# Gains of the inner norms folded into the split of the transposed output; modulation sums and a rotation product moved from GpSimd to VectorE

## The chip, the cores and the metric

One core of one Trainium2 chip runs the whole program once. The metric is the device time of that execution in microseconds (us): 1910.28 us before, the median of 3 runs (1908.68 to 1917.12). The engines are named as the profile names them: PE (TensorE matmuls), PEld (its weight loads), DVE (VectorE), ACT (ScalarE), POOL (GpSimd), SP (the queue that issues most DMAs).

## The reference, cut to what matters

Four layers run on 512 sample tokens and 128 prompt tokens of width 1024: differential attention, retention, HGRN2, differential attention. Every layer modulates its normed input, projects it, mixes it, norms each head, gates it and projects it back:

```python
for l in range(4):
    shift, scale, gate = split(silu(c) @ w_mod[l] + b_mod[l])   # for c and for c_ctx
    h = rms_norm(x, g_pre[l]) * (1 + scale) + shift
    # attention: q and k of the samples get the axial rotation
    #   x1*cos - x2*sin, x1*sin + x2*cos  on pairs of a head's 64 values
    o = rms_norm(o, da_subln[j]) * (1 - lam_init)    # layers 0 and 3, gain of 128, the same for 8 heads
    o = rms_norm(o)                                  # layer 1, no gain
    o = rms_norm(o, hg_norm)                         # layer 2, gain of 128, the same for 8 heads
    y = (o * silu(g)) @ w_out
    x = x + gate * rms_norm(y, g_post[l])
```

## The kernel before, in words

Activations stand transposed as `hh` and `hl` (8 blocks of 128 features by 640 tokens), a rounded high part and the low rest; weights are split in the same way into `whi` and `wlo`. A product is three matmuls (high by high, high by low, low by high). Each split costs a copy on ACT (the high part) and a subtraction on DVE or POOL (the low part, `lo`, L116).

The order of PE's instructions is written out by hand. In a layer, `weave` alternates the mixer of one head (`main`) with the projections of later heads (`fill`). All other queues (DVE, ACT, POOL, SP) are ordered by the framework's scheduler from its own estimates, so a change of any instruction can shift the order on these four; each queue then runs strictly in that order, so a waiting instruction holds whatever stands behind it.

Four pieces matter here.

**Modulation sums.** `mod_next` (L340 to L369) multiplies rows of `w_mod` into the accumulator `macc`, a row of 128 by 256 for each of two conditioning vectors. In the attention layers odd rows take this way: two ACT copies with a scale make `mpart` (L359, two buffers), and POOL adds it to `macc` (L363, 128 by 512). Even rows are two multiply-adds on DVE (L361). The sums are one chain: each step reads what the last one wrote. Layer 0 has 48 such adds, layer 3 has 16; in layer 1 all of it is on DVE, and layer 2 has none.

**Rotation.** `rope` (L750 to L768): DVE multiplies by the cosine (L757), swaps neighbours with a shuffle (L759), POOL multiplies by the sine (L761), DVE adds (L762), ACT makes the high part (L763), DVE the low (L764). DMAs then rearrange the keys into `kk` and `kz` (L735) and the queries into `qq` (L742), and PE scores them (L783, L784). This runs 32 times in each attention layer.

**Gate.** `gate` (L617 to L625) makes 2 silu(g) with ACT and DVE; in the attention layers and in HGRN2 a POOL product (L625) then multiplies the norm's gain in, from a tile that a DMA has broadcast to all partitions (`sub`, L655, scaled on DVE at L656; `ng`, L1061).

**Transposed output.** `head_out` (L627) scales a head's result by the reciprocal root from POOL (L391) and by the gate into `y` (L637). `y_to_h` (L440) and `y_col` (L492) transpose `y` by 128 columns, so that a head's 128 values lie on partitions, and split the result into `hh` and `hl`: ACT at L431 or L498, DVE at L116.

At the start `setup` loads small parameter rows by DMAs on ACT's queue (L280 to L286), transposes them on PE (L293, L302) and copies them into `par`.

Of the kernel before, what the change touches and what calls it, by code (L numbers as in the profile page):

```python
# [11 lines left out]
F32 = mybir.dt.float32  # L12
# [76 lines left out]
class Net:  # L89
# [187 lines left out]
    def setup(self, sp):  # L277
        nc, t, cp = self.nc, self.t, self.cp
        rows = sp.tile([96, 4, P], F32, name="rows")
        nc.scalar.dma_start(rows[0:8, 0, :], t["c"].rearrange("b (r p) -> (b r) p", p=P))  # L280
        self.ident = self.const(cp, "ident")
        nc.scalar.dma_start(rows[8:16, 0, :], t["c_ctx"].rearrange("(r p) -> r p", p=P))
        nc.scalar.dma_start(rows[:, 1, :], t["b_mod"].rearrange("l (r p) -> (l r) p", p=P))
        nc.scalar.dma_start(rows[0:32, 2, :], t["g_pre"].rearrange("l (r p) -> (l r) p", p=P))
        nc.scalar.dma_start(rows[32:64, 2, :], t["g_post"].rearrange("l (r p) -> (l r) p", p=P))
        nc.scalar.dma_start(rows[0:64, 3, :], t["hg_lb"].rearrange("d l (r p) -> (d l r) p", p=P))  # L286
        self.half = cp.tile([P, NT], F32, name="mhalf")
        nc.vector.memset(self.half, -0.5)
        self.smod = cp.tile([P, KT, 32], F32, name="smod")
        nc.vector.memset(self.smod, 0.0)  # L290
        par = cp.tile([P, 240], F32, name="par")
        pt = self.one()
        nc.tensor.transpose(pt[:, 0:16], rows[:16, 0, :], self.ident[:16, :16])  # L293
        nc.vector.tensor_copy(par[:, 0:16], pt[:, 0:16])
        th = sp.tile([P, 16], F32, name="th")
        nc.scalar.activation(th, par[:, 0:16], AF.Tanh, scale=0.5)
        nc.vector.scalar_tensor_tensor(out=th, in0=th, scalar=1.0, in1=par[:, 0:16], op0=ALU.add, op1=ALU.mult)
        nc.vector.tensor_scalar(out=self.smod[:, :, 0:2], in0=th.rearrange("p (j k) -> p k j", j=2),
                                scalar1=0.5, scalar2=None, op0=ALU.mult)
        pt = self.one()  # L300
        for i, n, o in ((1, 96, 0), (2, 64, 96), (3, 64, 160)):
            nc.tensor.transpose(pt[:, o:o + n], rows[:n, i, :], self.ident[:n, :n])  # L302
        nc.vector.tensor_copy(par[:, 16:240], pt[:, 0:224])
        self.bmodT = par[:, 16:112].rearrange("p (l r) -> p l r", l=4)
        self.gpre = par[:, 112:144].rearrange("p (l r) -> p l r", l=4)
        self.gpost = par[:, 144:176].rearrange("p (l r) -> p l r", l=4)
        self.lbl = par[:, 176:240].rearrange("p (d l r) -> p d l r", d=2, l=4)
# [33 lines left out]
    def mod_next(self, rows):  # L341
# [3 lines left out]
        while self.mod_owed >= 1 and self.modr:  # L345
# [16 lines left out]
            if pool is not None:  # L362
                nc.gpsimd.tensor_tensor(out=self.macc, in0=self.macc, in1=part, op=ALU.add)  # L363
            if 4 * i + k == 5:
# [62 lines left out]

    def put_h(self, src, tt, eng=None, k0=0):
        nc = self.nc
        hi, lo = (a[:, k0:k0 + src.shape[1], TOK[tt]:TOK[tt] + 128] for a in (self.hh, self.hl))  # L430
        nc.scalar.activation(hi, src, AF.Copy)  # L431
        self.lo(lo, src, hi, eng)

# [7 lines left out]
    def y_to_h(self, y, tt, n=KT, m=4):  # L441

        nc = self.nc
        for k0 in range(0, n, m):
            ks = range(k0, min(n, k0 + m))
            pt = self.one([P, 4, P]) if m == 4 else self.two([P, 8, P])
            for k in ks:
                nc.tensor.transpose(pt[:, k - k0, :], y[:, k * 128:k * 128 + 128], self.ident)
            self.put_h(pt[:, 0:len(ks), :], tt, nc.vector, k0)
            yield 0.11 * len(ks)  # L450
# [41 lines left out]
    def y_col(self, y, k):  # L492

        nc = self.nc
        pt = self.two([P, 1024])
        for tt in range(NT):
            nc.tensor.transpose(pt[:, TOK[tt]:TOK[tt] + 128], y[:, tt, k * 128:k * 128 + 128], self.ident)
        a = nc.scalar.activation(self.hh[:, k, :], pt[:, 0:640], AF.Copy)  # L498
        b = self.lo(self.hl[:, k, :], pt[:, 0:640], self.hh[:, k, :], nc.vector)
        return a.ins, b.ins  # L500
# [115 lines left out]

    def gate(self, o, ps, gain=None):  # L617

        nc = self.nc
        nc.scalar.activation(o, ps, AF.Tanh, scale=0.5)  # L620
        nc.vector.scalar_tensor_tensor(out=o, in0=o, scalar=1.0, in1=ps, op0=ALU.add, op1=ALU.mult)
        if gain is not None:
            n = 2 * o.shape[1]
            o = o.rearrange("p t (h e) -> p (t h) e", e=P)
            nc.gpsimd.tensor_tensor(out=o, in0=o, in1=gain.unsqueeze(1).to_broadcast([P, n, P]), op=ALU.mult)  # L625

# [18 lines left out]
    def diff(self, l, y):  # L645
# [3 lines left out]
        with tc.tile_pool(name=f"da{l}", bufs=2, reuse_waits="tile") as mp:  # L649
# [3 lines left out]
            nc.sync.dma_start(lv, t["da_lambda"][j].rearrange("a b -> (a b)").partition_broadcast(P))  # L653
            sub = mp.tile([P, P], F32, bufs=1, name="sub")
            nc.sync.dma_start(sub, t["da_subln"][j].partition_broadcast(P))  # L655
            nc.vector.tensor_scalar(out=sub, in0=sub, scalar1=1.0 - lam_init, scalar2=None, op0=ALU.mult)  # L656
            lp = mp.tile([P, 2, 64], F32, tag="sh", name="lp")
# [7 lines left out]
            nc.vector.tensor_scalar(out=nlam, in0=nlam, scalar1=-lam_init, scalar2=None, op0=ALU.add)  # L665
            st = types.SimpleNamespace(mp=mp, l=l, j=j, cc=cc, cs=cs, sub=sub, nlam=nlam, v={}, sg={}, q={}, k={})
            st.o, st.scored, st.done = {}, -1, -1
# [16 lines left out]
    def diff_part(self, st, kind, p):  # L684
# [13 lines left out]
        def use_g(tr, ps):  # L698
            self.gate(sg[:, tr, :], ps, st.sub)

# [49 lines left out]
    def rope(self, st, c0, hi, lo, pr, scale=1.0):  # L750
# [3 lines left out]
        def use(j, ps):  # L754
# [5 lines left out]
            nc.scalar.activation(pr[:, j * 64:j * 64 + 64], prompts(ps, j), AF.Copy, scale=scale)  # L760
            nc.gpsimd.tensor_tensor(out=sh, in0=sh, in1=st.cs[:, c], op=ALU.mult)  # L761
            nc.vector.tensor_tensor(out=t1, in0=t1, in1=sh, op=ALU.add)  # L762
# [287 lines left out]
    def hg(self, l, y):  # L1050
        nc, tc, t = self.nc, self.tc, self.t
        with tc.tile_pool(name=f"hg{l}", bufs=1, reuse_waits="tile") as mp:
# [3 lines left out]
            for m, n in ((mf, "mf"), (mg, "mg")):  # L1056
                c = mp.tile([P, 640], F32, tag="w0", bufs=5, name="w0")[:, 0:320]
                nc.sync.dma_start(c, t["consts"][:, CWHERE[n][0]:sum(CWHERE[n])])
                nc.vector.tensor_copy(m.rearrange("p a b -> p (a b)"), c)
            ng = mp.tile([P, P], F32, name="ng")  # L1060
            nc.sync.dma_start(ng, t["hg_norm"][0].partition_broadcast(P))  # L1061

# [23 lines left out]
            for z in pz:  # L1086
                nc.vector.memset(z, 0.0)
            st = types.SimpleNamespace(mp=mp, l=l, rs=rs, mf=mf, mg=mg, ng=ng, co=co, pz=pz, iv={}, sg={}, h={})
            for _ in self.hg_proj(st, 0):
# [7 lines left out]
    def hg_proj(self, st, h):  # L1097
        nc, t, mp = self.nc, self.t, st.mp
        if h == 0:
# [3 lines left out]
            def use(tt, ps):  # L1103
                nc.scalar.activation(iv[:, tt, :], ps[:, 0, :], AF.Copy)
                self.gate(sg[:, tt:tt + 1, :], ps[:, 1:2, :], st.ng)

# [6 lines left out]
        else:  # L1113
            p = h // 2
            sg = st.sg[p] = mp.tile([P, NT, 256], F32, tag="sg", bufs=2, name="sg")
            yield from self.narrow(st.l, 4096 + p * 256, lambda tr, ps: self.gate(sg[:, tr, :], ps, st.ng))
        hd = st.h[h] = types.SimpleNamespace(th=[])
# [315 lines left out]
```

## Time and profile before

| | |
|---|---|
| median of 3 runs | 1910.28 us |
| the profiled execution | 1908.83 us, its span 1907.0 us |
| granted clock of TensorE, mean | 0.989 |
| attention of layer 0, mostly | 55 to 400 us |
| retention | 500 to 945 us |
| HGRN2 | 1060 to 1410 us |
| attention of layer 3 | 1500 to 1825 us |

The span is from the first instruction to the last. A row such as `L363 POOL ... macc<-macc,mpart` names the line of the code, the engine, the tile written and the tiles read. "Idle before" is time in which that engine had nothing to run, with what ended it. The chain is followed back from the last instruction, at each step to what released it. An instruction's duration includes any time in which it stood started but blocked.

### The profile page before, as it was taken

To read this page: it belongs to the slowest core of one execution; us is meant where nothing else is said; L and a number is where in the kernel's file an instruction comes from. 1 tells how busy PE (TensorE), PEld (TensorE's weight loads), DVE (VectorE), ACT (ScalarE), POOL (GpSimd) and SP (SyncE) were. 2 spreads that over 40 slices of the span, in tenths; PEclk is the share of its full clock that TensorE was granted. 3 is DMA by queue.
4 is the path that set the end of the run, shared out by engine and by line. 5 is a ranking of instruction groups with operands and counts; after the bars stand their busy time and mean duration, and the time that the engine had idled before them with its cause. 6 is when DMAs were issued, how large, how long until landed. Compare 5 with 4: busy or idle time off the path is not lost.

```text
span 1907.0 us, 32063 instructions
## 1 busy us (share of the span) xinstructions
PE 1814.8 (95%) x12060; PEld 1651.2 (87%) x12060; DVE 1315.7 (69%) x2553; ACT 978.1 (51%) x2271; POOL 503.7 (26%) x419
## 2 busy tenths in 40 slices
PE   6989999999999999999999999999979989999998
PEld 4888999977888888888878899999978879999976
DVE  5768788857788998774334667676764766667754
ACT  3456666555444344433343456666654545655552
POOL 0414343202222222222101323342431521222101
PEclk9999999999999999999999999999989999999999
DMA  9644445414345445433323222222214463443322
GB/s 323 177 114 133 133 138 144 128 57 155 126 133 168 140 143 157 142 124 101 104 99 111 85 70 73 64 62 73 62 42 138 132 172 89 112 115 88 107 72 101
DMA packets 231963, 224.59 MB, mean 118 GB/s; under 512 B 11664, under 2 KB 201984, under 8 KB 231808
## 3 DMA queue, kind: packets, MB, share of 16 engines
q1 hardware_dynamic: 231344, 222.16, 38.7%
q8 instruction: 95, 1.56, 0.4%
q14 instruction: 60, 0.49, 0.1%
q10 hardware_dynamic: 464, 0.39, 0.1%
HBM read 174.79 MB, written 18.35 MB: 101 GB/s over the span
## 4 chain that ended last, share of the span: by engine, by line
PE 57%; DVE 20%; ACT 8%; DMA 5%; issue 4%; POOL 3%; SPq 2%; DVEq 0%; ACTq 0%; POOLq 0%
PE one L458 7%; PE one L460 7%; PE one L459 7%; PE one L250 4%; PE one L251 4%; PE one L252 4%; DVE macc L361 4%; DVE wlo L116 3%; PE one L821 3%; PE one L225 3%; PE one L226 2%; PE one L227 2%; ACT whi L178 2%; DMA kz<-ks 1%; DVE nm L785 1%
## 5 line engine op out<-in xcount | busy, mean ns | idle before, releaser
L250 PE MATMUL one<-hh,whi 128*128 128x320 f32 x1152 | 365.4, 317 | 9.3 <-ACT qp L760 6.4
L251 PE MATMUL one<-hl,whi 128*128 128x320 f32 x1152 | 357.0, 310 | 0.0
L252 PE MATMUL one<-hh,wlo 128*128 128x320 f32 x1152 | 356.8, 310 | 0.0
L116 DVE TENSOR_TENSOR wlo<-raw,whi 128x1024 fp32r<-128x1024 f32 x192 | 246.4, 1290 | 134.2 <-ACT whi L178 132.9
L458 PE MATMUL one<-whi,hh 128*128 128x512 f32 x744 | 303.0, 407 | 5.8 <-ACT yo L554 2.5
L460 PE MATMUL one<-whi,hl 128*128 128x512 f32 x744 | 296.1, 398 | 1.0 <-DVE hl L116 0.5
L459 PE MATMUL one<-wlo,hh 128*128 128x512 f32 x744 | 295.6, 397 | 0.0
L178 ACT ACTIVATE whi<-raw 128x1024 fp32r<-128x1024 f32 x192 | 201.3, 1056 | 138.4 <-PE one L251 52.0
L250 PEld LDWEIGHTS one<-hh,whi 128*128 128x128 f32 x1152 | 217.6, 189 | 12.0 <-ACT qp L760 6.8
L361 DVE SCALAR_TENSOR_TENSOR macc<-mraw,smod,macc 128x256 f32<-128x256 f32 x432 | 216.3, 544 | 10.2 <-POOL macc L363 9.6
L251 PEld LDWEIGHTS one<-hl,whi 128*128 128x128 f32 x1152 | 217.6, 189 | 0.5
L252 PEld LDWEIGHTS one<-hh,wlo 128*128 128x128 f32 x1152 | 217.3, 189 | 0.3 <-DVE wlo L116 0.3
L225 PE MATMUL one<-whi,hh 128*128 128x256 f32 x720 | 207.8, 289 | 0.0
L226 PE MATMUL one<-wlo,hh 128*128 128x256 f32 x720 | 201.1, 279 | 0.0
L227 PE MATMUL one<-whi,hl 128*128 128x256 f32 x720 | 201.1, 279 | 0.0
L458 PEld LDWEIGHTS one<-whi,hh 128*128 128x128 f32 x744 | 141.3, 190 | 38.5 <-DVE p L1007 4.0
L460 PEld LDWEIGHTS one<-whi,hl 128*128 128x128 f32 x744 | 140.8, 189 | 37.1 <-DVE hl L116 2.3
L459 PEld LDWEIGHTS one<-wlo,hh 128*128 128x128 f32 x744 | 141.3, 190 | 29.4
L363 POOL TENSOR_TENSOR macc<-macc,mpart 128x512 f32<-128x512 f32 x64 | 94.7, 1481 | 180.9 <-ACT macc L359 65.3
L391 POOL TENSOR_TENSOR rs<-ms,mhalf 128x1 f32<-128x1 f32 (+1 forms) x72 | 66.0, 917 | 288.3 <-DVE ms L384 152.9
L225 PEld LDWEIGHTS one<-whi,hh 128*128 128x128 f32 x720 | 135.5, 188 | 1.5
L226 PEld LDWEIGHTS one<-wlo,hh 128*128 128x128 f32 x720 | 135.6, 188 | 0.0
(344 smaller groups left out, 3765.0 us busy)
## 6 DMA issues: line engine op xcount, KB each, us to landing
mraw<-in_w_mod SPq DMA_DIRECT2D x96, 512.0 KB, 4.2
raw<-in_da_w_in SPq DMA_DIRECT2D x56, 512.0 KB, 4.2
raw<-in_hg_w_in SPq DMA_DIRECT2D x36, 512.0 KB, 3.8
raw<-in_ret_w_in SPq DMA_DIRECT2D x64, 256.0 KB, 3.1
kk<-ks SPq DMA_DIRECT2D x64, 160.0 KB, 3.4
kz<-ks SPq DMA_DIRECT2D x64, 160.0 KB, 3.2
qq<-q SPq DMA_DIRECT2D x64, 128.0 KB, 3.5
raw<-in_da_w_out SPq DMA_DIRECT2D x16, 512.0 KB, 3.5
```

The lines of the kernel that those rows point to most:

```text
L116: return (eng or self.nc.gpsimd).tensor_tensor(out=out, in0=full, in1=hi.bitcast(F32), op=ALU.subtract)
L178: self.nc.scalar.activation(hi, raw, AF.Copy)
L225: mm(out, xh, wh[:, k % 4, :], start=(first and k == ks[0]), stop=False)
L226: mm(out, xh, wl[:, k % 4, :], start=False, stop=False)
L227: mm(out, xl, wh[:, k % 4, :], start=False, stop=(last and k == ks[-1]))
L250: nc.tensor.matmul(ps, wh[:, k, :], self.hh[:, k, c], start=(k == 0), stop=False)
L251: nc.tensor.matmul(ps, wh[:, k, :], self.hl[:, k, c], start=False, stop=False)
L252: nc.tensor.matmul(ps, wl[:, k, :], self.hh[:, k, c], start=False, stop=(k == KT - 1))
L361: nc.vector.scalar_tensor_tensor(out=m, in0=raw[:, k, :], scalar=c, in1=m, op0=ALU.mult, op1=ALU.add)
L458: mm(ps, xh, wh, start=(first and k == ks[0]), stop=False)
L459: mm(ps, xh, wl, start=False, stop=False)
L460: mm(ps, xl, wh, start=False, stop=(last and k == ks[-1]))
```

## The change

Three edits. The gains `hg_norm` and `da_subln` are loaded as three more parameter rows at the head of ACT's DMA queue, transposed with the others, and become per-partition columns (`gains`); those of the attention are scaled by 1 - lam_init there. The POOL product in `gate` and the three broadcast tiles go; instead the split of the transposed output applies the gain, as the scale of ACT's copy and as the scalar of a DVE multiply-subtract. L363's add and L761's product are issued on DVE instead of POOL.

```diff
 def setup(self, sp):
+        nc.scalar.dma_start(rows[64:65, 3, :], t["hg_norm"])
+        nc.scalar.dma_start(rows[65:67, 3, :], t["da_subln"])
         nc.scalar.dma_start(rows[0:8, 0, :], t["c"].rearrange("b (r p) -> (b r) p", p=P))
...
-        for i, n, o in ((1, 96, 0), (2, 64, 96), (3, 64, 160)):
+        for i, n, o in ((1, 96, 0), (2, 64, 96), (3, 67, 160)):
...
+        self.gains = par[:, 240:243]
+        for l in (0, 3):
+            g = self.gains[:, 1 + SLOTS[l]:2 + SLOTS[l]]
+            nc.vector.tensor_scalar(out=g, in0=g, scalar1=1.0 - (0.8 - 0.6 * math.exp(-0.3 * l)), scalar2=None, op0=ALU.mult)
 def mod_next(self, rows):
-                nc.gpsimd.tensor_tensor(out=self.macc, in0=self.macc, in1=part, op=ALU.add)
+                nc.vector.tensor_tensor(out=self.macc, in0=self.macc, in1=part, op=ALU.add)
+    def cut_h(self, hi, lo, src, gain, eng):
+        if gain is None:
+            return self.nc.scalar.activation(hi, src, AF.Copy), self.lo(lo, src, hi, eng)
+        a = self.nc.scalar.activation(hi, src, AF.Copy, scale=gain)
+        return a, eng.scalar_tensor_tensor(out=lo, in0=src, scalar=gain, in1=hi.bitcast(F32), op0=ALU.mult, op1=ALU.subtract)
 def y_to_h(self, y, tt, n=KT, m=4):
-            self.put_h(pt[:, 0:len(ks), :], tt, nc.vector, k0)
+            self.put_h(pt[:, 0:len(ks), :], tt, nc.vector, k0, self.gain)
 def y_col(self, y, k):
-        a = nc.scalar.activation(self.hh[:, k, :], pt[:, 0:640], AF.Copy)
-        b = self.lo(self.hl[:, k, :], pt[:, 0:640], self.hh[:, k, :], nc.vector)
+        a, b = self.cut_h(self.hh[:, k, :], self.hl[:, k, :], pt[:, 0:640], self.gain, nc.vector)
 def gate(self, o, ps):
-        if gain is not None:
-            n = 2 * o.shape[1]
-            o = o.rearrange("p t (h e) -> p (t h) e", e=P)
-            nc.gpsimd.tensor_tensor(out=o, in0=o, in1=gain.unsqueeze(1).to_broadcast([P, n, P]), op=ALU.mult)
 def diff(self, l, y):
-            sub = mp.tile([P, P], F32, bufs=1, name="sub")
-            nc.sync.dma_start(sub, t["da_subln"][j].partition_broadcast(P))
-            nc.vector.tensor_scalar(out=sub, in0=sub, scalar1=1.0 - lam_init, scalar2=None, op0=ALU.mult)
+            self.gain = self.gains[:, 1 + j:2 + j]
 def rope(self, st, c0, hi, lo, pr, scale=1.0):
-            nc.gpsimd.tensor_tensor(out=sh, in0=sh, in1=st.cs[:, c], op=ALU.mult)
+            nc.vector.tensor_tensor(out=sh, in0=sh, in1=st.cs[:, c], op=ALU.mult)
 def hg(self, l, y):
-            ng = mp.tile([P, P], F32, name="ng")
-            nc.sync.dma_start(ng, t["hg_norm"][0].partition_broadcast(P))
+            self.gain = self.gains[:, 0:1]
```

In retention `gain` is None and the split stays as it was. `gate`'s callers drop the argument.

## Rows read from the trace of the kernel before

**Rows 1.** The page: busy time of each engine; the chain by engine.
```profile
PE 1814.8 (95%) x12060; PEld 1651.2 (87%) x12060; DVE 1315.7 (69%) x2553; ACT 978.1 (51%) x2271; POOL 503.7 (26%) x419
...
PE 57%; DVE 20%; ACT 8%; DMA 5%; issue 4%; POOL 3%; SPq 2%; DVEq 0%; ACTq 0%; POOLq 0%
```

**Rows 2.** Busy time by stretch: layer 0, HGRN2, layer 3; then clock, DMA share, GB/s.
```profile
55.00:400.00 345.00, 323.56 (x2366) 311.55 (x2365) 273.31 (x569) 207.95 (x582) 122.92 (x101) 0.99 0.48 136
...
1060.00:1410.00 350.00, 335.46 (x2770) 327.43 (x2771) 240.27 (x360) 218.12 (x425) 117.50 (x85) 0.99 0.23 69
...
1500.00:1825.00 325.00, 312.92 (x2329) 303.25 (x2328) 225.11 (x485) 178.53 (x493) 81.33 (x70) 1.00 0.43 116
```

**Rows 3.** The chain by line, in the stretch 55 to 400 us.
```profile
by line: issue 7.2%; PE one L821 6.9%; DMA kz<-ks 6.1%; DVE nm L785 5.4%; PE one L225 4.7%; PE one L227 4.3%; PE one L226 4.3%; DVE macc L361 3.9%; DVE wlo L116 3.8%; POOL macc L363 3.3%; ACT pe L787 2.9%; SPq L735 2.7%; PE one L811 2.3%; A
```

**Rows 4.** The same from 60 to 100 us and from 1505 to 1555 us.
```profile
by line: issue 13.6%; DMA qq<-q 12.5%; DMA raw<-in_da_w_in 9.7%; POOL sg L625 8.8%; DMA kz<-ks 7.6%; DMA v<-in_cache_v 7.2%; DVE t L762 6.9%; DVE macc L361 6.9%; DVE sh L759 4.5%; DVE wlo L116 4.2%; SPq L735 3.7%; POOL macc L363 3.3%; DVE t
...
by line: POOL macc L363 13.6%; issue 11.7%; DVE macc L361 8.3%; POOL sh L761 7.8%; DMA ck<-in_cache_k 7.2%; DMA mraw<-in_w_mod 6.9%; SPq L735 5.9%; DVE sh L759 5.3%; DVE wlo L116 4.7%; DVE t L757 3.9%; DVE t L762 3.3%; PE one L460 2.4%; PE 
```

**Rows 5.** POOL's groups, layer 0 then layer 3: count | busy us, mean ns | idle before.
```profile
L363 POOL TENSOR_TENSOR macc<-macc,mpart 128x512 f32<-128x512 f32 x48 | 70.3, 1465 | 155.2 <-ACT macc L359 59.3 <-ACT mpart L359 43.7 <-DVE macc L361 31.0
L761 POOL TENSOR_TENSOR sh<-sh,c_ropes 128x256 f32<-128x256 f32 x32 | 30.2, 946 | 67.0 <-DVE sh L759 49.0 <-DVE rc L861 17.9
...
L761 POOL TENSOR_TENSOR sh<-sh,c_ropes 128x256 f32<-128x256 f32 x32 | 34.1, 1065 | 117.8 <-DVE sh L759 64.0 <-DVE ms L389 31.8 <-DVE rc L861 19.0
L363 POOL TENSOR_TENSOR macc<-macc,mpart 128x512 f32<-128x512 f32 x16 | 24.4, 1527 | 25.7 <-DVE macc L361 11.1 <-ACT macc L359 6.0 <-DVE sub L656 5.1
```

**Rows 6.** Waits of ACT, layer 0: us in total, times, longest.
```profile
ACT mpart L359 <- POOL macc L363: 19.7, 20, 2.8
```

**Rows 7.** DVE's groups in layer 0: count | busy us, mean ns | idle before.
```profile
L116 DVE TENSOR_TENSOR wlo<-raw,whi 128x1024 fp32r<-128x1024 f32 x30 | 42.3, 1417 | 3.2 <-ACT whi L178 3.1
L361 DVE SCALAR_TENSOR_TENSOR macc<-mraw,smod,macc 128x256 f32<-128x256 f32 x72 | 35.6, 530 | 2.9 <-POOL macc L363 2.9
...
L762 DVE TENSOR_TENSOR t<-t,sh 128x256 f32<-128x256 f32 x32 | 20.5, 643 | 1.1 <-POOL sh L761 1.1
L862 DVE SCALAR_TENSOR_TENSOR rc<-sums,nlam,rc 128x1 f32<-128x1 f32 x36 | 16.2, 449 | 0.8
...
L116 DVE TENSOR_TENSOR hl<-one,hh 128x512 fp32r<-128x512 f32 x5 | 3.4, 682 | 0.0
```

**Rows 8.** Durations of four of these groups in layer 0: ns min/median/max, first and last start.
```profile
L116 DVE TENSOR_TENSOR wlo<-raw,whi x30: 1199/1221/2326, 59.3 to 383.6; 128x1024 fp32r<-128x1024 f32 x30
L361 DVE SCALAR_TENSOR_TENSOR macc<-mraw,smod,macc x72: 465/474/970, 62.5 to 343.9; 128x256 f32<-128x256 f32 x72
L762 DVE TENSOR_TENSOR t<-t,sh x32: 399/414/1532, 75.2 to 384.8; 128x256 f32<-128x256 f32 x32
L862 DVE SCALAR_TENSOR_TENSOR rc<-sums,nlam,rc x36: 203/220/1256, 105.8 to 396.0; 128x1 f32<-128x1 f32 x36
```

**Rows 9.** Groups of the whole run: a DVE sum of 640, ACT copies with and without scale.
```profile
L1150 DVE TENSOR_TENSOR w<-c 128x640 f32<-128x640 f32 x32 | 25.1, 820 | 0.8
...
L400 ACT ACTIVATE xh<-xt,rs 128x1024 f32<-128x1024 f32 x15 | 17.2, 1149 | 16.8 <-POOL rs L391 16.8
...
L398 ACT ACTIVATE xh<-xt 128x1024 f32<-128x1024 f32 x15 | 15.9, 1059 | 16.8 <-DVE xt L604 16.5
```

**Rows 10.** The gate's products on POOL, whole run.
```profile
L625 POOL TENSOR_TENSOR sg<-sg,sub 128x256 f32<-128x256 f32 (+1 forms) x28 | 28.6, 1027 | 79.9 <-DVE sg L621 71.5 <-DVE modT L334 6.5 <-DMA v<-in_cache_v 1.9
...
L625 POOL TENSOR_TENSOR sg<-sg,ng 128x256 f32<-128x256 f32 (+1 forms) x14 | 18.1, 1297 | 33.6 <-DVE sg L621 28.9 <-DVE lmx L1069 4.7
```

**Rows 11.** Timeline of the start: start us, us, instruction.
```profile
4.85 0.53 ACTq L286 DMA_DIRECT2D rows<-in_hg_lb  x1
...
10.43 0.36 PE L302 MATMUL one<-c_ident,rows 64*128 64x64 f32 x1 [2.42 <-DMA rows<-in_hg_lb]
...
17.08 1.93 PE L1288 MATMUL two<-mraw,smod 128*32 128x256 f32 x16 [2.74 <-DMA mraw<-in_w_mod]
```

More of the change, by code (lines that the diff above doesn't have):

```diff
@@ L290, in setup @@
         nc.vector.memset(self.smod, 0.0)
-        par = cp.tile([P, 240], F32, name="par")
+        par = cp.tile([P, 243], F32, name="par")
         pt = self.one()
@@ L300, in setup @@
         pt = self.one()
-        for i, n, o in ((1, 96, 0), (2, 64, 96), (3, 64, 160)):
+        for i, n, o in ((1, 96, 0), (2, 64, 96), (3, 67, 160)):
             nc.tensor.transpose(pt[:, o:o + n], rows[:n, i, :], self.ident[:n, :n])
-        nc.vector.tensor_copy(par[:, 16:240], pt[:, 0:224])
+        nc.vector.tensor_copy(par[:, 16:243], pt[:, 0:227])
+        self.gains = par[:, 240:243]
+        for l in (0, 3):
+            g = self.gains[:, 1 + SLOTS[l]:2 + SLOTS[l]]
+            nc.vector.tensor_scalar(out=g, in0=g, scalar1=1.0 - (0.8 - 0.6 * math.exp(-0.3 * l)), scalar2=None, op0=ALU.mult)
         self.bmodT = par[:, 16:112].rearrange("p (l r) -> p l r", l=4)
@@ L426, in enter, with put_h @@
         return step
-    def put_h(self, src, tt, eng=None, k0=0):
+    def put_h(self, src, tt, eng=None, k0=0, gain=None):
         nc = self.nc
         hi, lo = (a[:, k0:k0 + src.shape[1], TOK[tt]:TOK[tt] + 128] for a in (self.hh, self.hl))
-        nc.scalar.activation(hi, src, AF.Copy)
-        self.lo(lo, src, hi, eng)
+        self.cut_h(hi, lo, src, gain, eng)
+    def cut_h(self, hi, lo, src, gain, eng):
[3 more added lines that the diff above has]
+        return a, eng.scalar_tensor_tensor(out=lo, in0=src, scalar=gain, in1=hi.bitcast(F32), op0=ALU.mult, op1=ALU.subtract)
     def norm(self, pool, ssq):
@@ L614, in out_layer, with gate @@
                         self.turn(op, l + 1, tt + 3, xh[tt + 3])
-    def gate(self, o, ps, gain=None):
+    def gate(self, o, ps):
         nc = self.nc
@@ L665, in diff @@
             nc.vector.tensor_scalar(out=nlam, in0=nlam, scalar1=-lam_init, scalar2=None, op0=ALU.add)
-            st = types.SimpleNamespace(mp=mp, l=l, j=j, cc=cc, cs=cs, sub=sub, nlam=nlam, v={}, sg={}, q={}, k={})
+            st = types.SimpleNamespace(mp=mp, l=l, j=j, cc=cc, cs=cs, nlam=nlam, v={}, sg={}, q={}, k={})
             st.o, st.scored, st.done = {}, -1, -1
@@ L698, in use_g @@
         def use_g(tr, ps):
-            self.gate(sg[:, tr, :], ps, st.sub)
+            self.gate(sg[:, tr, :], ps)
         def use(tt, ps):
@@ L868, in ret @@
         with tc.tile_pool(name=f"re{l}", bufs=1, reuse_waits="tile") as mp:
+            self.gain = None
             rx = self.const(mp, "rx")
@@ L1087, in hg @@
                 nc.vector.memset(z, 0.0)
-            st = types.SimpleNamespace(mp=mp, l=l, rs=rs, mf=mf, mg=mg, ng=ng, co=co, pz=pz, iv={}, sg={}, h={})
+            st = types.SimpleNamespace(mp=mp, l=l, rs=rs, mf=mf, mg=mg, co=co, pz=pz, iv={}, sg={}, h={})
             for _ in self.hg_proj(st, 0):
@@ L1104, in use @@
                 nc.scalar.activation(iv[:, tt, :], ps[:, 0, :], AF.Copy)
-                self.gate(sg[:, tt:tt + 1, :], ps[:, 1:2, :], st.ng)
+                self.gate(sg[:, tt:tt + 1, :], ps[:, 1:2, :])
             yield from self.proj_a(st.l, 0, use)
@@ L1115, in hg_proj @@
             sg = st.sg[p] = mp.tile([P, NT, 256], F32, tag="sg", bufs=2, name="sg")
-            yield from self.narrow(st.l, 4096 + p * 256, lambda tr, ps: self.gate(sg[:, tr, :], ps, st.ng))
+            yield from self.narrow(st.l, 4096 + p * 256, lambda tr, ps: self.gate(sg[:, tr, :], ps))
         hd = st.h[h] = types.SimpleNamespace(th=[])
```

## The prediction

> **What bounds the kernel now.** I read the page first, then busy time by stretch, then the chain of the stretches that the edits touch, then the groups of POOL and DVE there, and last the spread of single DVE instructions.
>
> The page says that PE is busy for 95% of the span and carries 57% of the chain; DVE follows with 20%, and POOL has 3% [rows 1]. So the most that any edit off PE can return is PE's idle time in the stretches it touches. By stretch that is 345 - 323.56 = 21.4 us in layer 0, 325 - 312.92 = 12.1 us in layer 3 and 350 - 335.46 = 14.5 us in HGRN2 [rows 2]; 33.5 us in the two attention layers.
>
> Layer 0 differs from the other two: its chain is hardly PE. Its first entries are time in which nothing shown was waited for, the value products, the transfer of the keys (6.1%) and DVE's maximum; POOL's add L363 has 3.3% and DVE's half of the same sum 3.9% [rows 3]. In the two starts, POOL weighs more: the gate's product has 8.8% of the 40 us from 60 us on; the add 13.6% and the rotation's product 7.8% of the 50 us from 1505 us on [rows 4]. These are the pieces that the change takes away.
>
> Two further readings say why POOL is dear here. The add takes 1465 ns on average in layer 0, and ACT stands for 19.7 us before `mpart` until the add has freed one of its two buffers [rows 5, 6]; what stands behind it in ACT's queue (the copies that PE's value products need) stands as well. And DVE's instructions in layer 0 come in two kinds: the 128x1 scalar product L862 takes 220 ns as a median, 449 ns as a mean and 1256 ns at worst; L762 has 414, 643 and 1532 [rows 7, 8]. An instruction on one element doesn't take a microsecond by itself; about one POOL instruction is added to it.
>
> **The change part by part.** I make the sum against the profiled execution, 1908.83 us with a span of 1907.0; the median shown is 1.45 us above it.
>
> *POOL's pieces on the chain.* In layer 0 the add has 3.3% of 345 us = 11.4 us [rows 3]. In the start of layer 3 the add has 13.6% of 50 us = 6.8 us and the sine product 7.8% = 3.9 us; the gate's product has 8.8% of 40 us = 3.5 us in the start of layer 0 [rows 4]. Together 25.6 us.
>
> *What DVE takes for them.* The nearest row for an add of 128x512 is DVE's subtraction of the same size, 682 ns [rows 7]; its one operand from PSUM is the difference, and the bounds are 414 ns, the median for half the size from SBUF [rows 8], and 820 ns, the sum of 640 from SBUF [rows 9]. I take 682, the same size. The sine product is a DVE instruction of 128x256 like L762: 414 ns [rows 8], between 399, its minimum, and 682. So the 11.4 us become 11.4 x 682 / 1465 = 5.3, the 6.8 us become 6.8 x 682 / 1527 = 3.0, and the 3.9 us become 3.9 x 414 / 1065 = 1.5 [rows 5]; the gate's 3.5 us go altogether. The chain loses 25.6 - 9.8 = 15.8 us.
>
> [...]
>
> *DVE's load.* New on DVE are 48 + 16 adds, 64 x 0.682 = 43.6 us, and 32 + 32 products, 64 x 0.414 = 26.5 us: 70.1 us in all, 46.0 in layer 0 and 24.1 in layer 3. What DVE gets back is the time in which it stood blocked beside POOL. In layer 0, mean less median times count gives 30 x 196 = 5.9 us (weights' low part), 72 x 56 = 4.0 (L361), 32 x 229 = 7.3 (L762) and 36 x 229 = 8.2 (L862): 25.4 us in four groups [rows 7, 8]. For layer 3 I scale by POOL's moved time, (24.4 + 34.1) / (70.3 + 30.2) = 0.58 [rows 5], which gives 14.8 us, an estimate. So 40.2 us come back at least, bounds 0 (the spread has another cause) and 70 (smaller groups have it too). The load rises by 70.1 - 40.2 = 29.9 us; 9.8 of it is already counted on the chain, and the other 20.1 delay the chain at DVE's share of it, 20% [rows 1]: +4.0 us. DVE's busy time in layer 0 becomes 273.3 + 46.0 - 25.4 = 294 of 345 us [rows 2], 85% instead of 79%: still not the bound.
>
> [...]
>
> *Waits that go.* The 19.7 us of ACT before `mpart` [rows 6] become waits for DVE's add, shorter but behind DVE's queue. I count nothing for it: it is the margin against the next late thing, the transfer of the keys at 6.1% of layer 0's chain [rows 3], which no edit shortens.
>
> *The gate's product.* Off POOL go 28.6 us in the attention layers, counted above where they were on the chain, and 18.1 us in HGRN2 [rows 10]. There PE has 14.5 us of idle time in 350 us [rows 2]; I take a tenth, -1.5 us, between 0 and -5.
>
> *The split with a gain.* Per gained layer 12 splits (ten of `y_to_h`, two of `y_col`), 36 in all. ACT's copy with a column as scale costs 1149 - 1059 = 90 ns more [rows 9]; on DVE a multiply-subtract in place of a subtraction is bounded by 0 and, from L361's 474 ns against L762's 414, by 60 ns [rows 8]. At 150 ns together two or three splits of a layer are waited for by PE, the others run beside the mixer: 8 x 0.15 = +1.2 us. If none was covered it would be 36 x 0.15 = 5.4 us.
>
> *The start.* Two more DMAs stand ahead of `c` on ACT's queue, each about 0.5 us of issue by the 0.53 us of the last one; PE's third parameter transpose waits for that last one until 10.43 us [rows 11]. A delay of 1 us there is covered by PE's wait of 2.74 us for the modulation weights before 17.08 us [rows 11]. +0.5 us; if the cover was gone, 3. Two small DVE scalings and three DMAs less on SP, a scaling of `sub` less on DVE: one against the other, nothing, hidden behind the same transfers.
>
> Sum: -15.8 + 4.0 - 1.5 + 1.2 + 0.5 = -11.6, so 1908.8 - 11.6 = 1897.2: **1897 us**, 0.7% below the median.
>
> **The rivals.**
> - *PE and the keys' transfer hide it.* Layer 0's chain is made of many short pieces with a second one close behind; 95% of PE [rows 1] speaks for it. If two thirds of the 15.8 us are taken up by what is late next, -11.6 + 10.5 = -1.1: 1908 us. The starts of both layers, where POOL itself stands on the chain for microseconds, speak against it.
> - *The blocked time was on the chain.* The return of 40 us on DVE shortens pieces that lie on it now. If all 70 us of relief come and ACT's 19.7 us of waits count for a third, the +4.0 becomes 0 and 6.6 more go: -11.6 - 4.0 - 6.6 = -22.2, 1887 us, still within PE's 33.5 us of idle time.
> - *DVE waits in its own queue.* This ends slower. POOL could stand before an add until ACT had made both halves of `mpart` at no cost; DVE can't, for the scores' maximum and the combination stand behind the add, and PE behind those. POOL did stand: 59.3 and 43.7 us in layer 0 by ACT's copies [rows 5], though mostly where nothing was due. If each of 64 adds holds DVE for a time w, and half of that reaches the chain (layer 0 is 85% full), the price is 32 w. At w = 1 us, near the 1.06 us of an ACT copy [rows 9], it is +32: 1929 us; at w = 0.7 it is about +22 and the kernel is just slower by 0.5%. Against it: the scheduler knows ACT's work and can place the add after it.
> - *It doesn't do what it says.* The scheduler orders the four queues anew for the whole program, so layers that no edit touches can move by a few us either way. That alone gives 1904 to 1914 us.
>
> **How the numbers follow.** About 0.5%, 9.6 us, is what a measurement of this kernel can tell from no change: 1900.7 and 1919.8 us are the bounds of same. Forecast 0.45 (three quarters of it below 1900.7), blocked time on the chain 0.2, hidden 0.15, a new order alone 0.1, DVE waiting 0.1 (all of it slower by over 0.5%). Faster: 0.34 + 0.2 + a little of the rest = 0.57; slower 0.10; same 0.33. The range takes the second rival with the add at its lower bound (64 x 0.268 = 17.2 us less on DVE, 3.4 us at 20%) and HGRN2's -5 in place of -1.5, 1887 - 3.4 - 3.5 = 1880, and the hidden case with the uncovered start and splits, 1908 + 2.5 + 4.2 = 1914; left out are DVE waiting and some of both tails.
>
> **What would show it.** Right: no L363, L761 or L625 on POOL; the add near 682 ns and the product near 414 on DVE; L862's mean falling from 449 to under 260 ns; ACT's waits before `mpart` well under 19.7 us; PE's idle time in layers 0 and 3 down by 12 us together, HGRN2 by 1 or 2. Wrong: DVE idle before the add with ACT named as the releaser (the third rival); medians unchanged but the keys' transfer or SP's queue larger on layer 0's chain (the first); L862 still reaching a microsecond beside a POOL that runs nothing but L391.

## The result, and the profile after

The changed kernel takes 1884.26 us (median of 6 runs, 1880.94 to 1888.67), the kernel before 1912.47 beside it (6 runs, 1908.68 to 1917.12): a ratio of 0.9856, 95% interval 0.9839 to 0.9872. That is 28 us, faster as forecast, and inside the range. The profiled execution took 1885.44 us, with a span of 1883.7. The sum was made against the profiled execution before; the two lie 1908.83 - 1885.44 = 23.4 us apart, twice the 11.6 us of the sum.

The page after: busy time of each engine, and the chain by engine (compare [rows 1]).
```profile
PE 1804.6 (96%) x12060; PEld 1650.3 (88%) x12060; DVE 1304.6 (69%) x2681; ACT 980.7 (52%) x2271; POOL 300.2 (16%) x249
...
PE 66%; DVE 15%; ACT 7%; DMA 5%; issue 3%; SPq 2%; POOL 1%; DVEq 0%; ACTq 0%; POOLq 0%
```
POOL loses two fifths of its time. DVE's total does not rise although 128 instructions, some 70 us, are new on it, and its part of the chain falls from 20% to 15%.

Busy time by stretch (us, then PE, PEld, DVE, ACT, POOL with counts, granted clock, DMA share, GB/s): layer 0, the retention layer's middle, HGRN2, layer 3 (compare [rows 2]).
```profile
55.00:400.00 345.00, 338.48 (x2490) 324.39 (x2489) 280.05 (x675) 218.31 (x606) 8.17 (x7) 1.00 0.48 138
...
460.00:760.00 300.00, 289.05 (x1630) 255.69 (x1630) 257.18 (x565) 129.68 (x281) 81.35 (x58) 0.99 0.46 143
...
1060.00:1410.00 350.00, 337.52 (x2766) 329.29 (x2765) 234.82 (x367) 220.59 (x430) 97.46 (x69) 0.98 0.23 67
...
1500.00:1825.00 325.00, 318.65 (x2381) 309.50 (x2381) 229.09 (x539) 179.51 (x503) 8.18 (x7) 1.00 0.40 113
```
PE's idle time goes from 21.4 to 6.5 us in layer 0 and from 12.1 to 6.4 in layer 3. The chain of layer 0, where PE was hardly seen [rows 3], is now PE's matmuls:
```profile
by line: PE one L826 8.5%; PE one L225 8.0%; PE one L226 7.6%; PE one L227 7.6%; PE one L250 6.8%; PE one L251 6.7%; PE one L252 6.7%; PE two L788 4.8%; PE two L789 4.6%; PE one L816 4.1%; issue 3.8%; SPq L740 1.6%; DVE nm L790 1.5%; PE one
```

Single DVE instructions of layer 0 after: ns minimum/median/maximum, first and last start. The first two groups are the new ones; the other three answer to [rows 8] (the old L762, L862 and L361).
```profile
L369 DVE TENSOR_TENSOR macc<-macc,mpart x48: 676/685/695, 66.4 to 332.1; 128x512 f32<-128x512 f32 x48
L766 DVE TENSOR_TENSOR sh<-sh,c_ropes x32: 398/419/428, 78.4 to 366.6; 128x256 f32<-128x256 f32 x32
L767 DVE TENSOR_TENSOR t<-t,sh x32: 405/418/427, 81.4 to 368.4; 128x256 f32<-128x256 f32 x32
L867 DVE SCALAR_TENSOR_TENSOR rc<-sums,nlam,rc x39: 202/219/224, 108.0 to 398.7; 128x1 f32<-128x1 f32 x39
L367 DVE SCALAR_TENSOR_TENSOR macc<-mraw,smod,macc x72: 465/479/489, 67.1 to 330.3; 128x256 f32<-128x256 f32 x72
```
Medians stay, maxima fall onto them: the one-element product from 1256 ns to 224, L767 from 1532 to 427. Below, "blocked time" is what DVE's instructions of a stretch take above the shortest of their own kind, summed over all kinds. It goes from 48.6 to 8.4 us in layer 0 and from 22.0 to 6.1 in layer 3: 56 us returned. What the shortest instruction of a kind waits too is not in it.

Where the time comes from can be read without windows, since PE runs the same matmuls in the same order in every kernel here (one transpose of parameters at the start is three rows longer): the start of the k-th matmul against its start in the kernel before. These are single profiled executions, so the changed kernel ends 23.3 us ahead here, and not the 28 us of the medians.

| kernel | 250th (end of the start) | 500th | 2750th (end of layer 0) | 6250th (end of retention) | 9000th (end of HGRN2) | 11250th (end of layer 3) |
|---|---|---|---|---|---|---|
| changed | +5.3 | -0.6 | -16.2 | -15.6 | -16.8 | -24.1 |
| only the gain | +5.7 | +3.4 | +2.8 | -2.4 | -3.3 | -8.3 |
| only the sums | +0.3 | -4.1 | -11.4 | -10.6 | -9.5 | -15.6 |
| only the sine product | 0.0 | -1.0 | -1.4 | +0.7 | +0.2 | -3.8 |
| changed, idle sums on POOL | +5.1 | +4.9 | +0.8 | +1.4 | -1.5 | -5.5 |

The start loses 5.3 us, layer 0 then gains 21.5, retention and HGRN2 little, layer 3 another 7.3.

### The profile page after: what moved, and what is told of

Same layout as the page of the kernel before. It is cut to its first block, busy times and chain, and to the rows that moved or that the text cites. A ratio compares the mean times of both kernels' runs of the same rounds, so it can differ in the third digit from the quotient of the medians.

```text
span 1883.7 us, 31931 instructions
## 1 busy us (share of the span) xinstructions
PE 1804.6 (96%) x12060; PEld 1650.3 (88%) x12060; DVE 1304.6 (69%) x2681; ACT 980.7 (52%) x2271; POOL 300.2 (16%) x249
## 4 chain that ended last, share of the span: by engine, by line
PE 66%; DVE 15%; ACT 7%; DMA 5%; issue 3%; SPq 2%; POOL 1%; DVEq 0%; ACTq 0%; POOLq 0%
PE one L470 7%; PE one L472 7%; PE one L471 7%; PE one L250 5%; PE one L251 5%; PE one L252 5%; PE one L225 3%; PE one L826 3%; PE one L226 3%; PE one L227 3%; DVE macc L367 3%; DVE wlo L116 2%; PE two L788 2%; PE two L789 2%; PE one L816 1%
## 5 line engine op out<-in xcount | busy, mean ns | idle before, releaser
L116 DVE TENSOR_TENSOR wlo<-raw,whi 128x1024 fp32r<-128x1024 f32 x192 | 235.9, 1234 | 143.9 <-ACT whi L178 143.2
L367 DVE SCALAR_TENSOR_TENSOR macc<-mraw,smod,macc 128x256 f32<-128x256 f32 x432 | 209.1, 527 | 1.3 <-DMA mraw<-in_w_mod 1.1
L472 PEld LDWEIGHTS one<-whi,hl 128*128 128x128 f32 x744 | 141.0, 190 | 34.5 <-DVE hl L444 1.3
L227 PEld LDWEIGHTS one<-whi,hl 128*128 128x128 f32 x720 | 135.1, 188 | 0.0
```

The costliest lines, as they stand in the source:

```text
L116: return (eng or self.nc.gpsimd).tensor_tensor(out=out, in0=full, in1=hi.bitcast(F32), op=ALU.subtract)
L227: mm(out, xl, wh[:, k % 4, :], start=False, stop=(last and k == ks[-1]))
L367: nc.vector.scalar_tensor_tensor(out=m, in0=raw[:, k, :], scalar=c, in1=m, op0=ALU.mult, op1=ALU.add)
L472: mm(ps, xl, wh, start=False, stop=(last and k == ks[-1]))
```

## The experiments

**One part at a time.** Three kernels, each with one of the three edits. Only the gain: the changed kernel with both operations put back on POOL.
```diff
-                nc.vector.tensor_tensor(out=self.macc, in0=self.macc, in1=part, op=ALU.add)
+                nc.gpsimd.tensor_tensor(out=self.macc, in0=self.macc, in1=part, op=ALU.add)
...
-            nc.vector.tensor_tensor(out=sh, in0=sh, in1=st.cs[:, c], op=ALU.mult)
+            nc.gpsimd.tensor_tensor(out=sh, in0=sh, in1=st.cs[:, c], op=ALU.mult)
```


> The kernel before with the first edit alone: gains loaded first on ACT's queue and applied at the split, L363's add and the sine product still on POOL. Theory A (what counts is POOL's work standing on the chain): 2 to 6 us faster from the 46.7 us of products that leave POOL, less about 5 us that the start loses when two DMAs stand ahead of the conditioning vectors, so -4 to +3 us. Theory B (what counts is that DVE is blocked while POOL reads): the products block DVE too, so about the same, -5 to +2 us. The start in the trace tells the cost of the DMAs apart: +5 us at the last modulation matmul as in the full change, or 0 if that is another order of the queues.

Only the sums, in the kernel before (L363):
```diff
-                nc.gpsimd.tensor_tensor(out=self.macc, in0=self.macc, in1=part, op=ALU.add)
+                nc.vector.tensor_tensor(out=self.macc, in0=self.macc, in1=part, op=ALU.add)
```


> The kernel before with L363's 64 adds on DVE and nothing else. Theory A: most of the gain, 12 to 20 us, nearly all of it in layer 0 where 48 of them are. Theory B: the same size, but with DVE's block times down in proportion to POOL's time that goes (94.7 of 188 us), so 12 to 18 us. Rival (DVE waits in its own queue for ACT's two halves): slower, or DVE idle before the add by over 0.5 us each, 32 us.

Only the sine product, in the kernel before (L761):
```diff
-            nc.gpsimd.tensor_tensor(out=sh, in0=sh, in1=st.cs[:, c], op=ALU.mult)
+            nc.vector.tensor_tensor(out=sh, in0=sh, in1=st.cs[:, c], op=ALU.mult)
```


> The kernel before with the sine product on DVE and nothing else, 64 instructions. Theory A: 3 to 8 us faster, since POOL no longer holds the product behind an add; theory B: 2 to 6 us faster. If the order of the queues is what moves the time, layers 1 and 2 move as well, by over 3 us; both theories expect them unchanged within 2 us.

Measured: the gain alone 1904.39 us (ratio 0.9959, 0.9945 to 0.9972), the sums alone 1894.37 (0.9917, 0.9902 to 0.9931), the sine product alone 1901.25 (0.9952, 0.9933 to 0.997), beside 1910.27 for the kernel before. The gains of 5.9, 15.9 and 9.0 us add to 30.8, near the 28 of the whole, and the sums are the largest. The sums came out as expected; the gain and the sine product gained more than either theory allowed them, by a microsecond or more. Since both theories foresaw nearly the same sizes, these runs do not tell them apart. Nor are the parts clean prices: with the gain alone some 5 us are won in the retention layer (table), which that edit does not touch. In the kernel with the sums alone the one-element product of layer 0 reaches 692 ns at worst; with either of the others alone it still reaches 1256 or 1261.

**The place of the two new DMAs.** The changed kernel, with the two loads of gains last on ACT's queue instead of first.
```diff
-        nc.scalar.dma_start(rows[64:65, 3, :], t["hg_norm"])
-        nc.scalar.dma_start(rows[65:67, 3, :], t["da_subln"])
...
         nc.scalar.dma_start(rows[0:64, 3, :], t["hg_lb"].rearrange("d l (r p) -> (d l r) p", p=P))
+        nc.scalar.dma_start(rows[64:65, 3, :], t["hg_norm"])
+        nc.scalar.dma_start(rows[65:67, 3, :], t["da_subln"])
```


> The changed kernel with the two gain DMAs put last on ACT's queue, behind the one for the HGRN2 bounds. If the 5 us that the start loses come from the place of these DMAs, the last modulation matmul of the start comes 4 to 5 us earlier than in the changed kernel; the whole time falls by 4 to 5 us if the attention of layer 0 begins from there, and by under 1.5 us if that attention waits for its own transfers anyway. If it is a new order of DVE's queue at the start, nothing changes.

Measured: 1884.45 us (ratio 0.9863, 0.9849 to 0.9876), no difference from the changed kernel. The 250th matmul comes 3.1 us earlier than there, less than the 4 to 5 expected; of these, 1.5 us are left at the 275th, about as many at the 500th, and none from the 550th on (some 110 us into the run). So a delay of this size at the start is taken up before layer 0 is a third through; by what was not traced.

**ACT's wait without POOL's work moved.** The kernel before, with four buffers for `mpart` instead of two.
```diff
-                part = pool.tile([P, 2, 256], F32, tag="mpart", bufs=2, name="mpart")
+                part = pool.tile([P, 2, 256], F32, tag="mpart", bufs=4, name="mpart")
```


> The kernel before with four buffers of mpart instead of two, the adds still on POOL. It takes away ACT's wait of 19.7 us in layer 0 (and 6.5 us in layer 3) for POOL and leaves POOL's work and DVE's block times as they are. If ACT's wait is what the change took off the chain, 5 to 12 us faster; if it is DVE's block times, within 3 us of the kernel before.

Measured: 1912.85 us (ratio 1.0009, 0.9998 to 1.002). ACT's waits in layer 0 (us in total, times, longest) say why it settles nothing: the 19.7 us for POOL's sum [rows 6] are gone, and a wait for the modulation's weights stands in their place. The order on ACT's queue changed with the edit, and its copies now come ahead of their weights.
```profile
ACT mpart L359 <- DMA mraw<-in_w_mod: 28.2, 14, 5.2
```

**POOL's work without anyone waiting for it.** The changed kernel, with four buffers, and for each sum on DVE an idle one on POOL, into a tile that nobody reads; beside it the same with four buffers alone.
```diff
                 nc.vector.tensor_tensor(out=self.macc, in0=self.macc, in1=part, op=ALU.add)
+                junk = self.mod_pool.tile([P, 2, 256], F32, tag="mjunk", bufs=1, name="mjunk")
+                nc.gpsimd.tensor_tensor(out=junk, in0=part, in1=part, op=ALU.add)
```


> The changed kernel with four buffers of mpart and, beside each add on DVE, an add of the same size on POOL (mpart plus mpart) into a tile that nobody reads. The result is unchanged; POOL's 64 adds of about 1.3 us are back without anyone waiting for their result. If DVE's block times are what counts, L867 (the scalar product of one element) shows instructions of over 1 us again, DVE is busy for 25 us more in the attention layers, and the time is 6 to 14 us above the same kernel without those adds. If POOL's place on the chain is what counts, the two are within 2 us.

> The changed kernel with four buffers of mpart and nothing else, the base for the kernel with idle adds. Both theories: within 3 us of the changed kernel, since ACT's wait before mpart is already short there.

Measured: 1922.36 us with the idle sums (ratio 1.0057, 1.0036 to 1.0077), 1903.3 without (0.9959, 0.9946 to 0.9973). The control came out 19 us slower than the changed kernel, where at most 3 were expected. The same wait of ACT for weights is there (25.9 us in layer 0), but the order on DVE, ACT and SP moved as well, and in the kernel before, 28.2 us of this wait in place of 19.7 changed nothing; what made the 19 us was not shown. The pair still answers its question, since both have the same order on PE, DVE, ACT and SP: 19 us for POOL work that nobody waits for, more than the 6 to 14 expected. Layer 0 by stretch, with the idle sums and then without:
```profile
55.00:400.00 345.00, 317.90 (x2334) 305.77 (x2332) 285.24 (x640) 202.81 (x566) 64.53 (x54) 0.98 0.47 136
```
```profile
55.00:400.00 345.00, 326.07 (x2384) 313.67 (x2383) 272.04 (x654) 207.53 (x579) 7.06 (x6) 0.98 0.48 138
```
DVE is busy for 13 us more with fewer instructions done (640 for 654), and PE gets through 50 matmuls less.

**The same with nothing else changed.** The two buffers stay, and the idle sum reads the raw weights, so that the buffers of `mpart` come free as in the changed kernel. The buffer of the raw weights is now read by POOL too, but no queue is seen to wait for the idle sum, and ACT's waits for these weights in layer 0 are 2.9 us where the changed kernel has 2.3.
```diff
                 nc.vector.tensor_tensor(out=self.macc, in0=self.macc, in1=part, op=ALU.add)
+                for _ in range(1):
+                    junk = self.mod_pool.tile([P, 2, 256], F32, tag="mjunk", bufs=1, name="mjunk")
+                    nc.gpsimd.tensor_tensor(out=junk, in0=raw[:, k - 1:k + 1, :], in1=raw[:, k - 1:k + 1, :], op=ALU.add)
```


> The changed kernel with one thing more: for each of the 64 sums that went to DVE, POOL adds 128x512 elements of the modulation's raw weights to themselves, into a tile that nobody reads. The order of instructions on PE, DVE, ACT and SP is that of the changed kernel, and no engine waits for the sum. Theory B (POOL's work holds up DVE's instructions beside it, whoever waits for it): the single long DVE instructions come back (the 128x1 product of L867 over 1000 ns at worst), DVE's time above the shortest of each kind in layer 0 goes from 8 to some 30 us, and the kernel loses most of what the pair with four buffers lost for the same work, 19 us: about 1900 us, 1894 to 1906. Theory A (only waits for POOL's results counted): nobody waits, so 1884 us like the changed kernel, within 2.

Measured: 1898.63 us (ratio 0.9938, 0.992 to 0.9955), 14.4 us more than the changed kernel, whose interval lies wholly below. By the table above, layer 0 gives back 17.2 of its 21.5 us and layer 3 3.3 of its 7.3. Durations in layer 0 (minimum/median/maximum; lines are shifted by three):
```profile
L372 POOL TENSOR_TENSOR mjunk<-mraw x44: 1038/1102/2651, 74.1 to 329.1; 128x512 f32<-128x512 f32 x44
```
```profile
L369 DVE TENSOR_TENSOR macc<-macc,mpart x48: 668/681/1190, 66.2 to 348.9; 128x512 f32<-128x512 f32 x48
...
L870 DVE SCALAR_TENSOR_TENSOR rc<-sums,nlam,rc x36: 203/219/999, 111.9 to 396.9; 128x1 f32<-128x1 f32 x36
...
L367 DVE SCALAR_TENSOR_TENSOR macc<-mraw,smod,macc x72: 460/474/1321, 67.0 to 347.1; 128x256 f32<-128x256 f32 x72
```
The long instructions are back, with the order of PE, DVE, ACT and SP unchanged. Blocked time goes from 8.4 to 31.2 us in layer 0 and from 6.1 to 13.0 in layer 3. Theory A, which counts only waits for POOL's results, gave 1884 us and is out as the only cause.

Part of the cost shows as TensorE's clock. In layer 0 the granted clock is at half of full speed for 10.2 us in the kernel before, 3.4 in the changed one and 13.7 with the idle sums (0.99, 1.00 and 0.98 as the mean of the stretch); in the kernel before PE had stood idle for 2.4 to 2.6 us just ahead of each of its three falls, and 3.1 us of idle time at 80 us had no fall behind them. At half speed the 10.2 us that the idle sums add cost at most 5 us, an estimate from these figures.

One of the long instructions in the timeline of this kernel (start us, us, instruction):
```profile
185.20 2.96 POOL L372 TENSOR_TENSOR mjunk<-mraw 128x512 f32<-128x512 f32 x2 [7.95 <-DMA mraw<-in_w_mod]
...
185.75 0.41 DVE L635 SCALAR_TENSOR_TENSOR sg<-sg,one 128x256 f32<-128x256 f32 x1
...
186.08 1.19 DVE L369 TENSOR_TENSOR macc<-macc,mpart 128x512 f32<-128x512 f32 x1
...
187.19 0.99 DVE L870 SCALAR_TENSOR_TENSOR rc<-sums,nlam,rc 128x1 f32<-128x1 f32 x1
```
POOL's pair ends at 188.16 and the one-element product, which needs 0.22 us, at 187.19 + 0.99 = 188.18: it stands until POOL is done. The sum ahead of it, two inputs from SBUF too, stands for half a microsecond. L635, one of whose inputs is in PSUM, takes its usual 0.41 us in the middle of POOL's work. The kernel before shows the same at the sum L363, with a reciprocal of one input that passes unhindered:
```profile
177.30 1.31 POOL L363 TENSOR_TENSOR macc<-macc,mpart 128x512 f32<-128x512 f32 x1 [2.42 <-DVE macc L361]
...
177.36 0.16 DVE L861 RECIPROCAL rc<-sums 128x1 f32<-128x1 f32 x1 [0.21 <-ACT pe L787]
...
177.56 1.06 DVE L862 SCALAR_TENSOR_TENSOR rc<-sums,nlam,rc 128x1 f32<-128x1 f32 x1
```
Two groups of the kernel before part in the same way over all of layer 0. The rotation's sum L762 has two inputs in SBUF: where a POOL instruction runs beside it (12 of 32) it takes 1029 ns on average, elsewhere 411. The product by the cosine L757, of the same size, has one input in PSUM; 15 of its 32 instances run beside POOL, and none is long (compare L762 in [rows 8]):
```profile
L757 DVE TENSOR_TENSOR t<-one,c_ropec x32: 396/414/426, 71.5 to 381.2; 128x256 f32<-128x256 f32 x32
```
The place of the inputs does not explain every case: one instance of L336, with a single input in SBUF, takes 1287 ns there beside a gate's product on POOL and ends 0.03 us after it, where its median is 164. The traces show which instructions stand beside POOL and for how long; by what they are held was not shown.

**The same move elsewhere.** If POOL's work holds DVE up elsewhere too, more of it is worth moving. Nine low parts of 128x1024 from `turn`:
```diff
-        self.put_h(h, tt, nc.vector if tt in (0, 4) else None)
+        self.put_h(h, tt, nc.vector)
```


> The changed kernel, with the low part of the normalised input that POOL still makes for nine tiles of 128x1024 (hl of L116 by turn, 2519 ns each, 22.7 us) on DVE as well, at some 1.22 us each. Theory B: DVE gains 11 us of work but loses the long instructions beside POOL (L418, L615 and L367 of 2 to 3 us at worst); the exits of layers 0 and 2 have little idle PE time, so 1881 to 1884 us. Rival (DVE's load there sets the end): 1885 to 1888 us.

All low parts, the retention layer's too (`lo`, L116):
```diff
-        return (eng or self.nc.gpsimd).tensor_tensor(out=out, in0=full, in1=hi.bitcast(F32), op=ALU.subtract)
+        return (eng or self.nc.vector).tensor_tensor(out=out, in0=full, in1=hi.bitcast(F32), op=ALU.subtract)
```


> As the run with turn's low parts, and also the retention layer's four kinds of low parts (qd, kt, pw, states) on DVE instead of POOL: 54 us of new DVE work in place of 115 us on POOL. DVE in the 300 us of that layer is busy for 257, of which 26 us are above the shortest of each kind; it would be at 275 to 285. Theory B as the only cause: PE's idle time there (11 us in that stretch) shrinks and the kernel gets to 1874 to 1882 us. Rival (DVE's own queue becomes the bound once it is over 90% full, so the rule has an end): 1886 to 1896 us.

HGRN2's four products and sums (L1156):
```diff
-        DV, PL = nc.vector, nc.gpsimd
+        DV, PL = nc.vector, nc.vector
```


> The changed kernel with the HGRN2 mixer's four products and sums on POOL (64 instructions, 92 us there) on DVE: about 47 us of new DVE work in 350 us where DVE has 235, and 11 to 20 us of blocked time back. Theory B: PE's 12.5 us of idle time in that stretch shrink, 1877 to 1882 us. Rival (DVE waits in order for ACT's exponentials where POOL stood for them at no cost, 158 us by the waits, and everything behind stands as well): 1890 to 1910 us.

Both of these edits together:

> The changed kernel with both: all low parts and HGRN2's four products and sums on DVE; POOL keeps only the square roots' powers and the 20 copies of 128x512. Theory B with independent stretches: the two gains add, 1884.3 - 5.8 - 9.4 = 1869 us, within 2. Rival (the order of the queues is set anew for the whole program, and part of either gain is that order's): 1872 to 1880 us.

Measured, beside the changed kernel's 1884.26: `turn` 1881.48 us (ratio 0.9847, 0.9827 to 0.9868, not to be told from it), all low parts 1878.43 (0.9826, 0.9808 to 0.9844), HGRN2 1874.83 (0.9807, 0.9789 to 0.9826), both 1867.65 (0.9766, 0.9749 to 0.9784). All low parts lie just below the changed kernel, HGRN2 and the pair clearly so, and 1884.3 - 5.8 - 9.4 = 1869 foresaw the pair. The rival of a full queue on DVE was not put to the test: with all low parts DVE is busy for 265 of the 300 us from 460 us on. HGRN2 was better than its expectation, and its rival, that DVE would stand for ACT's exponentials as POOL did for 158 us, did not come: DVE's waits there for ACT before its L1155 instructions are 1.7 us. Two DVE groups of HGRN2 in the changed kernel, and the same with POOL's products moved to DVE:
```profile
L1155 DVE TENSOR_TENSOR of<-k,w 128x320 f32<-128x320 f32 x16 | 24.8, 1550 | 3.4 <-ACT w L1197 3.4
L1155 DVE TENSOR_TENSOR of<-q,w 128x320 f32<-128x320 f32 x16 | 24.3, 1521 | 0.0
```
```profile
L1155 DVE TENSOR_TENSOR of<-q,w 128x320 f32<-128x320 f32 x16 | 7.7, 484 | 0.0
L1155 DVE TENSOR_TENSOR of<-k,w 128x320 f32<-128x320 f32 x16 | 7.7, 483 | 0.0
```
These two groups alone return 49.1 - 15.4 = 33.7 us; the moved work is 47. They were slow in every one of 16 instances, so minimum and median hid it (869 and 1279 ns at best); only the price of the size, some 480 ns, shows it. With the move waits for POOL's results end too (ACT's before L1211, 10.0 us in the changed kernel); their part of the 9.4 us was not separated. The best kernel by the page and by stretch:
```profile
PE 1794.7 (96%) x12060; PEld 1641.7 (88%) x12060; DVE 1324.9 (71%) x2826; ACT 980.7 (53%) x2271; POOL 96.1 (5%) x104
...
460.00:760.00 300.00, 293.82 (x1682) 260.68 (x1681) 265.78 (x621) 132.10 (x284) 18.54 (x11) 0.99 0.47 149
...
1060.00:1410.00 350.00, 342.39 (x2874) 333.44 (x2873) 241.15 (x422) 223.90 (x442) 9.36 (x8) 0.99 0.24 71
```
Against the kernel before, POOL does 408 us less and DVE's busy time is 9 us more.

## Why the prediction was right, and where its sum was not

**The direction and the price of the pieces: right.** The sum was forecast at 682 ns and took 685, the sine product at 414 and took 419. ACT's waits before `mpart` for the sum fell from 19.7 us to this:
```profile
ACT mpart L365 <- DVE macc L369: 4.1, 5, 1.9
```
**The mechanism that counted was that of the rival "the blocked time was on the chain", 1887 us**; 1884.26 was measured. That the two numbers are so close is in part luck: the 1887 took 70 us of relief, near the 48.6 + 22.0 us of blocked time in the two attention layers before, and a third of ACT's waits, while 56 us of relief were measured and the share of ACT's waits was not separated. The forecast itself, 1897 us, was 13 us off, and the range held because its lower end, 1880, was made from this rival.

The step that failed is the term for DVE's load, +4.0 us. It netted 40.2 us of returned time against 70.1 of new work and charged the rest at DVE's share of the chain. Two things were off in it. The returned time measured 56 us. And one microsecond of it need not be worth the same as one of new work: 14.4 us of time came with 29.8 us of blocked time in the run with idle sums, 0.48 for each, and 19.1 with 31.1 in the pair with four buffers, 0.61. A reason is argued, not shown: a blocked instruction stands where POOL happens to run, ahead of things that the chain waits for, while the order of new work is chosen. A corrected sum can't be given. With 56 x 0.48 = 26.9 returned, (70.7 - 9.8) x 20% = 12.2 for the new work that the chain's pieces don't hold yet, and the other terms as forecast (-15.6), it would be -30.3; with 0.61 it would be -37.6; 23.4 us lie between the profiled executions. So some of these terms are too large or hold the same time twice: what POOL's pieces, ACT's wait and the new work each weigh was not separated.

**PE's idle time as the most that can return: wrong.** PE's busy time itself fell, from 1814.8 [rows 1] to 1804.6 us for the same 12060 matmuls, so 10.2 of the 23.3 us between the two spans lie in time that the profile counts as busy. The 6.8 us less of lower clock in layer 0 make up to 3.4 of them, an estimate; the rest was not followed up.

**DVE waits in its own queue: did not come.** DVE's idle time before L369 is 0.7 us in all, over 64 sums. **Hidden by the keys' transfer: did not come**; the chain of layer 0 passed to PE instead. **A new order alone** is seen in the kernel with only the gain: 5.2 us of its gain lie in the retention layer, which that edit does not touch; in the changed kernel retention ends within a microsecond of where it began.

**The gate in HGRN2**: forecast -1.5, measured -1.2 between the 6250th and the 9000th matmul. That agrees, but proves little: with the sums alone, which leave HGRN2 as it is, the same stretch moves by +1.1. **The split with a gain**: DVE's multiply-subtract of 128x512 takes 743 ns for 682 [rows 7], the upper bound of 60; ACT's scale costs 707 for 604 ns. Rows of the whole run after, and of the kernel before:
```profile
L444 DVE SCALAR_TENSOR_TENSOR hl<-one,par,hh 128x512 fp32r<-128x512 f32 x15 | 11.1, 743 | 0.3 <-ACT hh L443 0.2
...
L443 ACT ACTIVATE hh<-one,par 128x512 fp32r<-128x512 f32 x15 | 10.6, 707 | 1.6 <-PE one L460 1.6
```
```profile
L431 ACT ACTIVATE hh<-one 128x512 fp32r<-128x512 f32 x25 | 14.4, 604 | 3.6 <-PE one L448 3.6
```
**The start** was mis-sized: +0.5 us, 3 without cover, and 5.3 were measured. Not ACT's queue alone was late (L304 at 11.21 us instead of 10.43 [rows 11]): DVE's copy of the parameters, L305, was placed behind other work, at 14.34 us, where it stood at 11.41 in the kernel before.
```profile
14.34 0.39 DVE L305 COPY par<-one 128x227 f32<-128x227 f32 x1
```
The forecast looked for cover in PE's wait for the modulation weights, and that did not hold: the 400th matmul is still 5.1 us late. The table's -0.6 at the 500th does not show cover either, since the sums alone gain 4.4 us in that stretch; with idle sums on POOL the 500th still stands at +4.9. That 3.1 of the 5.3 us cost the end nothing is shown by the run with the loads placed last; of the rest it stays open.

## What to carry to other kernels

Read a group's minimum, median and maximum, and the price that its size has elsewhere, before reading its mean: here a one-element instruction of 1256 ns where 220 was its median, and products that averaged 1521 and 1550 ns where 483 and 484 were their price once POOL's work beside them had moved, were instructions held up while POOL worked. POOL work that nobody waited for cost 14.4 and 19 us here, and work that takes DVE about half as long as POOL (685 for 1465 ns, 419 for 946) was no worse on DVE in any move tried, and better in all but one, even though DVE looked the busier of the two. To test it, put idle work back and leave every queue's order as it is; that isolates what a change of buffers, which moved the order too, could not.

## What was not expected of the hardware

Moved to DVE, the work was nearly free there: 408 us less on POOL for 9 us more on DVE in the best kernel. Of the 408, 46.7 us were the gate's products [rows 10], which the split took over. In the window of HGRN2, which lies over 20 us later in the best kernel's work than in the old one's, DVE is busy for 241.2 us instead of 240.3 [rows 2], with 64 instructions of POOL's added. POOL's own instructions spread as well: the idle sum takes 1038 ns at best and 2651 at worst. ACT's hardly do: its instructions of layer 0 lie 7.6, 8.1 and 8.0 us above the shortest of their kinds in the kernel before, the changed one and the one with idle sums. And more buffers were not harmless: four for `mpart` cost the changed kernel 19 us. ACT's copies then stand for weights that have not arrived, and the order of three queues moved; which of the two made the 19 us is not shown.
